# A decoder layer on one core: 192 gathered tokens in place of 160, one-hot rows made four tokens at a time, and three pieces of work moved

## The chip, the core and the metric

The kernel runs on one core of a Trainium2 chip. Its engines are PE (TensorE, matrix products), DVE (VectorE), ACT (ScalarE), POOL (GpSimd) and SP (SyncE, which here only issues transfers); DMA engines move data between the main memory and the core's on-chip memory. The metric is the device time of one execution in microseconds (us), lower is better.

## What is computed

One layer of a decoder on 512 tokens of width 2048, in float32: two attention mixers with a gated merge, a layer norm, then a retrieval over 16,384 single-neuron experts, then a second layer norm. The part that the change touches is the retrieval. Cut to that:

```python
def peer_ffn(h, wq, subkeys, u_tab, v_tab):           # h: 512 x 2048, u_tab and v_tab: 16384 x 2048
    q = (xt @ wq).reshape(T, 8, 2, 128)
    s = einsum('thcd,hcnd->thcn', q, subkeys)           # scores against 128 keys, two halves, 8 heads
    top_s, top_i = top_k(s, 16)
    best_s, best_c = top_k(sums of the two halves' 16 x 16 candidates, 16)
    expert = i1 * 128 + i2                              # 8 x 16 = 128 experts of each token
    gate = softmax(best_s)
    act = gelu(einsum('cd,chkd->chk', xc, u_tab[expert]))
    return einsum('chk,chkd->cd', gate * act, v_tab[expert])
h1 = layer_norm(alpha * x + mix)
x  = layer_norm(alpha * h1 + peer_ffn(h1) + sigmoid(h1 @ ple_gate) * (p @ ple_proj))
```

## The kernel before

All large products are made three times from float32 split into a high and a low part: `mm3` (line 100) issues hi*hi, hi*lo and lo*hi into one sum. `load_split` (line 87) brings 512 KB of weights by SP, makes the high part `whi` on ACT (line 93) and the low part `wlo` on DVE (line 95), or on POOL (line 97) where that is asked for. The three tiles `raw`, `whi` and `wlo` have three buffers each.

The retrieval is done in two ways. For the first T0 = 128 + GX tokens (GX = 32, so 160) each token's 128 experts are **gathered**: 160 columns `k` of expert numbers (HG), one indirect transfer of 128 rows of 2048 floats (1 MB) for each, first from the u table, then from the v table, so 320 steps, and two more that only use what is there. A step (`gather_to`, line 624) issues the transfer of row tile n on POOL's queue (line 599) and lets DVE use row tile n-2: for u a product with the tokens and a sum (line 606), for v a multiply-add into `accg` or `accx` (line 620). There are three row tiles. For the other TD = 352 tokens the retrieval is **dense**: all 16,384 experts are computed for every one of them. The experts come in 128 units of 128; `dense_u` (line 712) makes one unit's products with 48 matmuls whose moving operand has TD columns. Eight units are a group; each result is multiplied by its gate (line 870), split again into `ah` and `al` (lines 873, 874), and the group's product with the v table (line 898) is 384 matmuls of TD columns, whose sums DVE adds into `acc` (line 902). There are 16 groups. The first 32 units' u products (LOOK = 4 groups) are made early, stored in `ad` and fetched again by POOL's queue into tiles `a` (line 866, two buffers).

The work around it, in the order of the program: the output projection `mix`, in two halves of 256 tokens, with the first layer norm of half 0 (`norm1(0)`) after the first four steps of the second half; `half_keys(0)` and `half_keys(1)`, the key search, with dense units in between as filler and, in the second, the first gather steps; `dense_gates` (line 654), which for each dense token makes a 128 x 128 table of gates as the product of two one-hot matrices, 16 tokens to a batch; two filler units and two gather steps go into each batch, the filler being first what is left of the early dense units, then the 32 units of `ple_units`. After that come the last eight of the 32 early units and the groups. `gather_steps` (line 800) spreads the gather steps that are left over 226 calls in the groups. At the end the sums are transposed, added and normalized.

A scheduler sets the order of the instructions on every engine from the program's order and its own estimates of times. `gather_to` asks it to place a step's instructions behind the latest `wlo` on DVE.

## Time and profile before

| what | us |
| --- | --- |
| median of three runs | 4023.78 (4021.25 to 4023.92) |
| profiled execution | 4021.22 |
| its span, first to last instruction | 4019.4 |
| PE busy | 3822.7 (95%) |
| DVE busy | 2704.3 (67%) |
| ACT busy | 1282.2 (32%) |
| POOL busy | 685.3 (17%) |

DMA moved 886.99 MB, on the mean 221 GB/s. A matmul is pipelined, so the duration shown for one (326 ns) is longer than the distance from one to the next; where PE runs without a gap the distance is read from the count of matmuls in a stretch. The profile's rows by stage tell more than the shares of the whole span, since the stages have different limits.

### The profile page before, as it was taken

The page shows a single profiled execution, that of the slowest core. Times are in us where ns is not written, and L with a number is a line of the kernel's source. Part 1 is how long each engine was busy: PE and PEld are TensorE (multiplying, and loading weights), DVE is VectorE, ACT ScalarE, POOL GpSimd, SP SyncE. Part 2 cuts the span into 40 slices and gives each one's busy share as a digit, 9 for nine tenths or more (in the row PEclk, how much of TensorE's full clock was granted, in tenths as well). Part 3 has the DMA queues.
Part 4 walks back from the last instruction along what each step waited for, and adds up shares of the span by engine and source line. Part 5 has one row for each costly group of instructions (what it writes and reads, how often), then busy time and mean ns, then how long its engine had stood idle before and what let it go on. Part 6 is the DMA issues. An engine that isn't in the chain of part 4 may idle for free.

```text
span 4019.4 us, 54040 instructions
## 1 busy us (share of the span) xinstructions
PE 3822.7 (95%) x21545; PEld 3535.9 (88%) x21545; DVE 2704.3 (67%) x4220; ACT 1282.2 (32%) x1660; POOL 685.3 (17%) x493
## 2 busy tenths in 40 slices
PE   8999999999998889979988899999999999999996
PEld 7888877888886789978878898999999999999996
DVE  5344343222257788899996777777777777777877
ACT  3222233222233433334433222333333333333331
POOL 0000000000002355521122222222211211111110
PEclk9999999999999999989998999999999999999998
DMA  4222222222256455658888787888888888888884
GB/s 141 95 89 85 76 74 71 92 95 94 95 190 191 155 163 181 226 199 281 287 292 303 270 304 287 304 324 310 302 323 303 310 316 298 316 310 306 318 300 152
DMA packets 242941, 886.99 MB, mean 221 GB/s; under 512 B 23040, under 2 KB 76416, under 8 KB 198016
## 3 DMA queue, kind: packets, MB, share of 16 engines
q1 hardware_dynamic: 182672, 499.91, 36.8%
q0 software_dynamic: 52672, 375.15, 25.5%
q10 hardware_dynamic: 7344, 8.47, 0.6%
q8 instruction: 169, 2.77, 0.3%
q14 instruction: 84, 0.69, 0.1%
HBM read 841.24 MB, written 41.42 MB: 220 GB/s over the span
## 4 chain that ended last, share of the span: by engine, by line
PE 81%; DVE 11%; DMA 3%; issue 3%; ACT 1%; POOL 1%; POOLq 0%; DVEq 0%; ACTq 0%; SPq 0%
PE hp L101 8%; PE hp L103 8%; PE hp L102 8%; PE vp L101 7%; PE vp L103 7%; PE vp L102 7%; PE ps_g L101 3%; PE ps_g L102 3%; PE ps_g L103 3%; PE pg L673 2%; DVE row L606 2%; PE pg L101 1%; PE pg L102 1%; PE pg L103 1%; DMA a<-ad 1%
## 5 line engine op out<-in xcount | busy, mean ns | idle before, releaser
L101 PE MATMUL vp<-ah,whi_vd 128*128 128x352 f32 x2048 | 657.5, 327 | 29.1 <-ACT ah L873 18.2
L103 PE MATMUL hp<-m_hi,wlo_u 128*128 128x352 f32 x2048 | 665.2, 325 | 20.4 <-DVE wlo_u L95 13.6
L101 PE MATMUL hp<-m_hi,whi_u 128*128 128x352 f32 x2048 | 668.4, 326 | 0.0
L102 PE MATMUL hp<-m_lo,whi_u 128*128 128x352 f32 x2048 | 662.5, 323 | 0.0
L102 PE MATMUL vp<-al,whi_vd 128*128 128x352 f32 x2048 | 662.1, 325 | 0.3 <-DVE al L874 0.3
L103 PE MATMUL vp<-ah,wlo_vd 128*128 128x352 f32 x2048 | 644.7, 326 | 9.8 <-DVE wlo_vd L95 9.8
L93 ACT ACTIVATE whi_vd<-raw_vd 128x1024 fp32r<-128x1024 f32 x256 | 270.4, 1059 | 671.5 <-PE vp L102 469.7
L93 ACT ACTIVATE whi_u<-raw_u 128x1024 fp32r<-128x1024 f32 x256 | 271.0, 1059 | 525.6 <-PE hp L102 309.1
L101 PEld LDWEIGHTS vp<-ah,whi_vd 128*128 128x128 f32 x2048 | 387.8, 191 | 33.6 <-ACT ah L873 20.1
L95 DVE TENSOR_TENSOR wlo_vd<-raw_vd,whi_vd 128x1024 fp32r<-128x1024 f32 x256 | 312.5, 1221 | 142.6 <-ACT whi_vd L93 142.3
L95 DVE TENSOR_TENSOR wlo_u<-raw_u,whi_u 128x1024 fp32r<-128x1024 f32 x236 | 295.3, 1252 | 165.6 <-ACT whi_u L93 164.9
L103 PEld LDWEIGHTS hp<-m_hi,wlo_u 128*128 128x128 f32 x2048 | 386.3, 189 | 22.4 <-DVE wlo_u L95 15.3
L103 PEld LDWEIGHTS vp<-ah,wlo_vd 128*128 128x128 f32 x2048 | 385.5, 190 | 11.2 <-DVE wlo_vd L95 11.2
L102 PEld LDWEIGHTS hp<-m_lo,whi_u 128*128 128x128 f32 x2048 | 390.1, 190 | 0.0
L102 PEld LDWEIGHTS vp<-al,whi_vd 128*128 128x128 f32 x2048 | 388.4, 190 | 0.9 <-DVE al L874 0.8
L101 PEld LDWEIGHTS hp<-m_hi,whi_u 128*128 128x128 f32 x2048 | 388.0, 189 | 0.0
L599 POOL DMA_INDIRECT row<-in_u_rows,eidx x160 | 204.1, 1276 | 816.6 <-DVE row L606 546.8
L599 POOL DMA_INDIRECT row<-in_v_rows,eidx x160 | 193.3, 1208 | 829.7 <-DVE accg L620 648.3
L620 DVE SCALAR_TENSOR_TENSOR accg<-row,act,accg 128x2048 f32<-128x2048 f32 x128 | 300.3, 2346 | 0.4
L606 DVE SCALAR_TENSOR_TENSOR row<-row,h1g 128x2048 f32<-128x2048 f32 x128 | 293.4, 2300 | 0.0
L511 POOL TENSOR_TENSOR h1g<-h1g,lnb 128x2048 f32<-128x2048 f32 x1 | 4.6, 4619 | 1259.5 <-PE ht L499 1259.5
L101 PE MATMUL ps_g<-x_hi,whi_g 128*128 128x512 f32 x512 | 202.9, 396 | 0.0
(332 smaller groups left out, 7387.4 us busy)
## 6 DMA issues: line engine op xcount, KB each, us to landing
raw_u<-in_u_dense SPq DMA_DIRECT2D x256, 512.0 KB, 5.5
raw_vd<-in_v_dense SPq DMA_DIRECT2D x256, 512.0 KB, 5.6
raw_g<-in_w_z SPq DMA_DIRECT2D x64, 512.0 KB, 3.4
raw_wo<-in_w_out SPq DMA_DIRECT2D x64, 512.0 KB, 4.2
raw_wq<-in_w_q SPq DMA_DIRECT2D x64, 512.0 KB, 4.0
gd<-sg SPq DMA_DIRECT2D x22, 1024.0 KB, 7.9
gl<-gd POOLq DMA_DIRECT2D x16, 1408.0 KB, 9.7
raw_pg<-in_w_gate SPq DMA_DIRECT2D x32, 512.0 KB, 5.4
```

What stands on the lines that cost most here:

```text
L93: nc.scalar.activation(hi[:, :n], raw[:, :n], AF.Copy)
L95: last_lo[0] = nc.vector.tensor_sub(lo[:, :n], raw[:, :n], hi[:, :n])
L101: nc.tensor.matmul(ps, whi, mhi, start=start, stop=False, **kw)
L102: nc.tensor.matmul(ps, whi, mlo, start=False, stop=False, **kw)
L103: nc.tensor.matmul(ps, wlo, mhi, start=False, stop=stop, **kw)
L511: nc.gpsimd.tensor_mul(o, o, lnb[:, 0, :])
L599: nc.gpsimd.indirect_dma_start(out=row, out_offset=None, in_=u_rows if n < HG else v_rows, in_offset=bass.IndirectOffsetOnAxis(ap=eidx[:, ...
L606: nc.vector.scalar_tensor_tensor(row, row, 1.0, state["h"][n >= HK], op0=ALU.mult, op1=ALU.mult, accum_out=act[:, n:n + 1])
L620: nc.vector.scalar_tensor_tensor(o, row, act[:, k:k + 1], o, op0=ALU.mult, op1=ALU.add)
L673: nc.tensor.matmul(ps[:, t1 * P:(t1 + 1) * P], o1, o2, start=True, stop=True)
```

## The change

GX goes from 32 to 64, so 192 tokens are gathered (384 row tiles, 386 steps) and 320 are dense (TD = 320). In `dense_gates` the one-hot rows are made four tokens at a time by one comparison each on DVE, and the gate is multiplied in by ACT, one instruction to a token; in each batch three gather steps are issued in place of two. `norm1(0)` is drawn out: its first part stands where all of it stood, its four transposing parts each after three steps of the second half of `mix`. Four of the early dense units (`fill(4)`) go between the key search and the gates. The tiles `a` have four buffers in the last of the early units and in the groups.

```diff
--- before.py
+++ after.py
@@ -22,7 +22,7 @@
 D = 2048
 KB = D // P
 NT = T // P
-GX = 32
+GX = 64
 GE = 8
 T0 = P + GX
 TD = T - T0
@@ -517,9 +517,12 @@
     rest = mix(1)
     for _ in range(4):
         next(rest)
-    for _ in norm1(0):
-        pass
-    for _ in rest:
+    early = norm1(0)
+    next(early)
+    for n, _ in enumerate(rest):
+        if n % 3 == 2:
+            next(early, None)
+    for _ in early:
         pass
 
     pre_q = [load_split(w_q[0][:, u * 1024:(u + 1) * 1024], f"wq0_{u}") for u in range(2)]
@@ -663,17 +666,23 @@
             for t4 in range(4):
                 ps = bank(f"pg{tb}_{b}_{t4}")
                 t0 = b * 16 + t4 * 4
+                def onehot(row, name):
+                    eq = k3.tile([P, 4, P], F32, tag=name, name=f"{name}{tb}_{t0}", bufs=2)
+                    nc.vector.tensor_tensor(
+                        eq, tt[:, row, t0:t0 + 4].unsqueeze(2).to_broadcast([P, 4, P]),
+                        io.unsqueeze(1).to_broadcast([P, 4, P]), op=ALU.is_equal)
+                    return eq
+
+                o1 = onehot(0, "o1")
+                eq = onehot(1, "eq")
                 for t1 in range(4):
                     t = t0 + t1
-                    o1 = k3.tile([P, P], F32, tag="o1", name=f"o1_{tb}_{t}", bufs=8)
-                    nc.vector.tensor_scalar(o1, io, tt[:, 0, t:t + 1], None, op0=ALU.is_equal)
                     o2 = k3.tile([P, P], F32, tag="o2", name=f"o2_{tb}_{t}", bufs=8)
-                    nc.vector.tensor_scalar(o2, io, tt[:, 1, t:t + 1], tt[:, 2, t:t + 1],
-                                            op0=ALU.is_equal, op1=ALU.mult)
-                    nc.tensor.matmul(ps[:, t1 * P:(t1 + 1) * P], o1, o2, start=True, stop=True)
+                    nc.scalar.activation(o2, eq[:, t1, :], AF.Copy, scale=tt[:, 2, t:t + 1])
+                    nc.tensor.matmul(ps[:, t1 * P:(t1 + 1) * P], o1[:, t1, :], o2, start=True, stop=True)
                 if t4 % 2:
                     fill(1)
-                    gather_to(steps[1] + 1)
+                    gather_to(steps[1] + (1 if t4 == 1 else 2))
                 nc.scalar.activation(sg[:, :, t4 * 4:(t4 + 1) * 4].rearrange("p i t -> p t i"),
                                      ps.rearrange("p (t i) -> p t i", i=P), AF.Copy)
             nc.sync.dma_start(gdw[:, :, tb * 8 + b - T0 // 16, :], sg.rearrange("p (g i) t -> p g (i t)", i=GE))
@@ -723,7 +732,7 @@
 
     def look_units(i, pool, n, share):
         for i2 in range(i, i + n):
-            a = pool.tile([P, TD], F32, tag="a", name=f"au{i2}")
+            a = pool.tile([P, TD], F32, tag="a", name=f"au{i2}", bufs=4 if pool is not fpool[0] else 2)
             dense_u(i2, a, share())
             nc.sync.dma_start(ad[i2 // GE][:, i2 % GE, :], a)
             yield
@@ -785,6 +794,7 @@
         yield from ple_units()
 
     units = gate_filler()
+    fill(4)
     for tb in range(1, NT):
         dense_gates(tb)
     fill(32 + LOOK * GE)
@@ -861,7 +871,7 @@
         if g:
             gt = gate_tile(g)
         for e in range(GE):
-            a = ap2.tile([P, TD], F32, tag="a", name=f"a{g}_{e}")
+            a = ap2.tile([P, TD], F32, tag="a", name=f"a{g}_{e}", bufs=4)
             if g < LOOK:
                 nc.gpsimd.dma_start(a, ad[g][:, e, :])
             else:
```

DVE between the key search and the first gates, before: the last lookups (`oh`, `ix`), the transposed indices (`tt`) and the first one-hot rows (`o`).

```order
L574 TENSOR_TENSOR oh_3_0_13295<-bcf_3_13293,io 128x512
L574 TENSOR_TENSOR oh_3_1_13299<-bcf_3_13293,io 128x512
L577 TENSOR_TENSOR oh_3_0_13295<-oh_3_0_13295,tf_3_13288 128x512
L577 TENSOR_TENSOR oh_3_1_13299<-oh_3_1_13299,tf_3_13288 128x512
L579 TENSOR_REDUCE ix<-oh_3_0_13295 128x32
L579 TENSOR_REDUCE ix<-oh_3_1_13299 128x32
L660 COPY tt_13335<-pit_13331 128x384
L669 TENSOR_SCALAR o_1_32_13339<-io,tt_13335 128x128
L671 TENSOR_SCALAR o_1_32_13341<-io,tt_13335 128x128
L669 TENSOR_SCALAR o_1_33_13344<-io,tt_13335 128x128
L671 TENSOR_SCALAR o_1_33_13346<-io,tt_13335 128x128
```

The same place now:

```order
L95 TENSOR_TENSOR wlo_u_1_13552<-raw_u_1_13549,whi_u_1_13551 128x1024
L577 TENSOR_TENSOR oh_3_0_13289<-bcf_3_13287,io 128x512
L577 TENSOR_TENSOR oh_3_1_13293<-bcf_3_13287,io 128x512
L580 TENSOR_TENSOR oh_3_0_13289<-oh_3_0_13289,tf_3_13282 128x512
L580 TENSOR_TENSOR oh_3_1_13293<-oh_3_1_13293,tf_3_13282 128x512
L95 TENSOR_TENSOR wlo_pg_0_13630<-raw_pg_0_13627,whi_pg_0_13629 128x1024
L609 SCALAR_TENSOR_TENSOR row_13086,act<-row_13086,h1g 128x2048
L582 TENSOR_REDUCE ix<-oh_3_0_13289 128x32
L582 TENSOR_REDUCE ix<-oh_3_1_13293 128x32
L95 TENSOR_TENSOR wlo_pg_1_13699<-raw_pg_1_13696,whi_pg_1_13698 128x1024
L609 SCALAR_TENSOR_TENSOR row_13233,act<-row_13233,h1g 128x2048
L609 SCALAR_TENSOR_TENSOR row_13657,act<-row_13657,h1g 128x2048
```

The low parts of dense units (`wlo_u`), of the next filler (`wlo_pg`) and gather steps (`row`) stand among the lookups.

POOL's queue at the border of two of the first groups, before: fetched units (`a`), a group's gates (`gl`) and row tiles (`row`).

```order
L866 DMA a_3_18114<-ad 128x352
L866 DMA a_4_18121<-ad 128x352
L599 DMA row_18216<-in_u_rows,eidx 128x2048
L599 DMA row_18283<-in_u_rows,eidx 128x2048
L866 DMA a_5_18128<-ad 128x352
L866 DMA a_6_18135<-ad 128x352
L599 DMA row_18350<-in_u_rows,eidx 128x2048
L866 DMA a_7_18142<-ad 128x352
L866 DMA a_0_18693<-ad 128x352
L853 DMA gl_18691<-gd 128x2816
```

The same border now:

```order
L876 DMA a_3_17668<-ad 128x320
L602 DMA row_17301<-in_u_rows,eidx 128x2048
L602 DMA row_17368<-in_u_rows,eidx 128x2048
L602 DMA row_17435<-in_u_rows,eidx 128x2048
L876 DMA a_4_17675<-ad 128x320
L602 DMA row_17438<-in_u_rows,eidx 128x2048
L602 DMA row_17505<-in_u_rows,eidx 128x2048
L602 DMA row_17572<-in_u_rows,eidx 128x2048
L602 DMA row_17639<-in_u_rows,eidx 128x2048
L602 DMA row_17642<-in_u_rows,eidx 128x2048
L602 DMA row_17767<-in_u_rows,eidx 128x2048
L876 DMA a_5_17682<-ad 128x320
```

At this border the later fetches of a group stood in ones and twos with one or two row tiles between them; now the fourth tile stands ahead of three row tiles, the fifth ahead of six more, and the sixth (`a_5`) behind these.

DVE in the u half of one of the later groups, before: low parts, gated results (`a`, `al`) and row tiles into `accg`.

```order
L95 TENSOR_TENSOR wlo_u_1_26764<-raw_u_1_26761,whi_u_1_26763 128x1024
L620 SCALAR_TENSOR_TENSOR accg<-row_26723,act,accg 128x2048
L874 TENSOR_TENSOR al_0_26649<-a_0_26584,ah_0_26648 128x352
L95 TENSOR_TENSOR wlo_u_0_26805<-raw_u_0_26802,whi_u_0_26804 128x1024
L870 TENSOR_TENSOR a_1_26655<-a_1_26655,gl_26582 128x352
L874 TENSOR_TENSOR al_1_26720<-a_1_26655,ah_1_26719 128x352
L95 TENSOR_TENSOR wlo_u_1_26835<-raw_u_1_26832,whi_u_1_26834 128x1024
L620 SCALAR_TENSOR_TENSOR accg<-row_26726,act,accg 128x2048
L95 TENSOR_TENSOR wlo_u_0_26876<-raw_u_0_26873,whi_u_0_26875 128x1024
```

The same place of a later group now:

```order
L95 TENSOR_TENSOR wlo_u_1_26319<-raw_u_1_26316,whi_u_1_26318 128x1024
L623 SCALAR_TENSOR_TENSOR accg<-row_26208,act,accg 128x2048
L95 TENSOR_TENSOR wlo_u_0_26363<-raw_u_0_26360,whi_u_0_26362 128x1024
L623 SCALAR_TENSOR_TENSOR accg<-row_26281,act,accg 128x2048
L880 TENSOR_TENSOR a_1_26284<-a_1_26284,gl_26211 128x320
L95 TENSOR_TENSOR wlo_u_1_26393<-raw_u_1_26390,whi_u_1_26392 128x1024
L623 SCALAR_TENSOR_TENSOR accg<-row_26352,act,accg 128x2048
L95 TENSOR_TENSOR wlo_u_0_26434<-raw_u_0_26431,whi_u_0_26433 128x1024
L884 TENSOR_TENSOR al_1_26349<-a_1_26284,ah_1_26348 128x320
L95 TENSOR_TENSOR wlo_u_1_26464<-raw_u_1_26461,whi_u_1_26463 128x1024
L623 SCALAR_TENSOR_TENSOR accg<-row_26355,act,accg 128x2048
```

In a later group 19 row tiles stood on DVE beside 32 low parts, 16 gated results and 16 sums; now 22 or 23 do, the rest is unchanged in number.

## Rows read from the trace of the kernel before

**Rows 1.** Busy time by stage: PE, PEld, DVE, ACT, POOL, clock, DMA share, GB/s.

```profile
1240.00:1310.00 70.00, 54.94 (x241) 43.37 (x240) 53.46 (x62) 26.45 (x37) 22.66 (x10) 0.90 0.60 185
1450.00:1750.00 300.00, 287.82 (x2060) 286.04 (x2060) 250.55 (x720) 109.22 (x149) 165.18 (x72) 0.98 0.62 199
1750.00:1790.00 40.00, 14.85 (x78) 14.30 (x77) 35.05 (x120) 8.70 (x11) 1.89 (x2) 0.66 0.40 135
1790.00:2080.00 290.00, 279.63 (x1519) 242.81 (x1518) 262.98 (x676) 120.19 (x126) 41.33 (x47) 0.98 0.86 283
2080.00:2140.00 60.00, 46.55 (x207) 39.60 (x207) 58.01 (x163) 23.21 (x24) 18.28 (x14) 0.72 0.84 300
2140.00:2200.00 60.00, 59.62 (x375) 59.33 (x373) 37.68 (x33) 20.99 (x25) 12.68 (x10) 1.00 0.87 322
2200.00:2495.00 295.00, 260.43 (x1528) 254.64 (x1529) 214.12 (x266) 81.14 (x97) 71.47 (x73) 0.95 0.77 283
2495.00:3920.00 1425.00, 1425.00 (x8874) 1425.00 (x8873) 1106.77 (x1027) 473.32 (x566) 280.00 (x231) 1.00 0.85 311
```

**Rows 2.** Timeline of PE, first and last of 48 matmuls of 256 columns.

```profile
1609.18 0.28 PE L101 MATMUL ps_wq<-m_hi,whi_wq 128*128 128x256 f32 x1
...
1614.76 0.28 PE L103 MATMUL ps_wq<-m_hi,wlo_wq 128*128 128x256 f32 x1
```

**Rows 3.** Groups by form, 2510 to 3910: count, busy us, mean ns, idle us.

```profile
L620 DVE SCALAR_TENSOR_TENSOR accg<-row,act,accg 128x2048 f32<-128x2048 f32 x128 | 300.3, 2346 | 0.4
L95 DVE TENSOR_TENSOR wlo_u<-raw_u,whi_u 128x1024 fp32r<-128x1024 f32 x187 | 228.6, 1223 | 106.1 <-ACT whi_u L93 105.6
L902 DVE TENSOR_TENSOR acc<-acc,vp 128x352 f32<-128x352 f32 x176 | 88.7, 515 | 59.9 <-PE vp L103 59.9
L874 DVE TENSOR_TENSOR al<-a,ah 128x352 fp32r<-128x352 f32 x93 | 48.7, 524 | 40.1 <-ACT ah L873 40.1
L599 POOL DMA_INDIRECT row<-in_v_rows,eidx x160 | 193.3, 1208 | 829.7 <-DVE accg L620 648.3 <-DVE accx L620 141.8 <-DMA row<-in_v_rows,eidx 13.0
```

**Rows 4.** DMA, 2510 to 3910: packets; gather queue; landing time of a row tile.

```profile
DMA packets 85119, 434.34 MB, mean 310 GB/s; under 512 B 9464, under 2 KB 9464, under 8 KB 55935
q0 software_dynamic: 32737, 242.64, 47.3%
row<-in_v_rows,eidx POOLq DMA_INDIRECT x160, 7.7
```

**Rows 5.** Timeline at the first norm: start, duration, engine, line.

```profile
1260.78 4.62 POOL L511 TENSOR_TENSOR h1g<-h1g,lnb 128x2048 f32<-128x2048 f32 x1 [1259.46 <-PE ht L499]
1266.40 4.83 DVE L505 TENSOR_TENSOR m_lo<-ht,m_hi 128x256 fp32r<-128x256 f32 x1
1271.76 8.74 DVE L505 TENSOR_TENSOR m_lo<-ht,m_hi 128x256 fp32r<-128x256 f32 x2
```

**Rows 6.** One-hot rows by form, comparison of 512 elements, ACT on 128 columns.

```profile
L671 DVE TENSOR_SCALAR o<-io,tt 128x128 f32<-128x128 f32 x336 | 113.8, 339 | 0.0
L669 DVE TENSOR_SCALAR o<-io,tt 128x128 f32<-128x128 f32 x336 | 93.8, 279 | 11.3 <-PE pg L673 11.2
1768.77 1.24 DVE L574 TENSOR_TENSOR oh<-bcf,io 128x512 f32<-128x512 f32 x2
L260 ACT ACTIVATE p<-p,nm 128x128 f32<-128x128 f32 x32 | 12.4, 387 | 0.0
```

**Rows 7.** Waits, 2190 to 2460: us in total, times, longest.

```profile
PE vp L101 <- ACT ah L873: 18.2, 6, 5.0
POOL row L599 <- DVE row L606: 137.7, 26, 8.3
DVE a L870 <- DMA a<-ad: 33.9, 8, 7.5
```

**Rows 8.** DMA, 2140 to 2200: landing time of a row tile.

```profile
row<-in_u_rows,eidx POOLq DMA_INDIRECT x8, 9.1
```

**Rows 9.** Busy time in ten us of the output projection, columns as in 1.

```profile
1150.00:1160.00 10.00, 10.00 (x45) 8.11 (x44) 2.46 (x3) 2.12 (x2) 0.00 (x0) 1.00 1.00 404
```

## The prediction

> **What bounds the kernel now.** I read first the busy time by stage [rows 1], then the groups of one stage by form, then the waits where PE is not full. From 2495 to 3920 PE is busy for all of 1425 us at the full clock; DVE has 1106.77 us of work there (78%) and DMA moves 311 GB/s at a share of 0.85. This stage, most of groups 4 to 15, is bound by PE alone, and two other engines have about a fifth and a seventh to spare. Ahead of it PE is not full: it lacks 15 us of the 70 at the first norm (1240 to 1310), 25 of the 40 between key search and gates (1750 to 1790, at a clock of 0.66), 10 and 13 us in the gates (1790 to 2140), and 35 of the 295 in the first groups (2200 to 2495). In the key search (1450 to 1750) DVE is busy for 250.55 of 300 us and PE for 287.82. So a shorter product is worth its full size only after 2140, and up to the point at which DVE or DMA is full.
>
> **The columns.** In the PE-bound stage 8874 matmuls of 352 columns take 1425 us, 160.6 ns each [rows 1]. At 256 columns, 47 distances take 1614.76 - 1609.18 = 5.58 us, 118.7 ns [rows 2]. The line between the two gives 146.6 ns at 320 columns: 14.0 ns less. No weight load stands in the way down to 256. There are 128 units of 48 and 16 groups of 384 such matmuls, 12,288 in all, so at most 12,288 x 14.0 ns = 172 us. By stage: 960 matmuls in the key search (13 us), the four moved units (192, 3 us), the last eight early units with groups 0 to 3 (1920, 27 us), groups 4 to 15 (9216, 129 us).
>
> **What the 64 further steps cost.** A step is 2.35 us of DVE [rows 3] (2.28 and a read of the sum for u rows) and 1.05 MB of DMA: 64 x 2.35 = 150 us and 67 MB. 16 of them fall into the gates, the rest behind. None is on PE; what they cost is what they take from the two spare shares.
>
> **Groups 4 to 15.** A group is 768 matmuls: 768 x 160.6 ns = 123.3 us now, 112.6 after. DVE in a group after: 32 low parts x 1.223 = 39.1; 16 sums x 0.48 = 7.7 and 16 gated results x 0.49 = 7.8 (0.515 and 0.524 now [rows 3], shortened by a sixteenth, since 32 of 352 columns go); 22.4 row tiles x 2.35 = 52.6. Sum 107.2 of 112.6 us, 95%. Before it is 39.1 + 8.2 + 8.3 + 19 x 2.35 = 100 of 123. DMA after: 32 loads of 0.524 MB = 16.8, 22.4 rows = 23.5, a gate tile 1.3, together 41.6 MB, which in 112.6 us is 369 GB/s. The mean of 310 GB/s [rows 4] at a share of 0.85 [rows 1] gives 365 GB/s at a full share, so 41.6 MB need 114 us; ten us of the output projection show 404 GB/s at a full share [rows 9], which gives 103. Row tiles: three buffers, and a buffer's round is the issue on POOL with the landing, 7.7 us [rows 4], 1.21 us of POOL [rows 3] ahead of it and 2.35 us of use: 11.3 us for three rows, 3.8 us a row, while 112.6 / 22.4 = 5.0 is allowed. But landing takes 9.1 us where 322 GB/s move [rows 8, 1]; at 11.5 us it is 22.4 x 15.05 / 3 = 112.4, the bound itself. So four limits lie between 103 and 114 us, and a queue that is full to 95% on three engines does not run at its bound. Bounds of a group: 113 (PE and a us of stalls) and 123 (nothing gained). I take 117, nearest to the DMA row at its own share. 12 x (123.3 - 117) = **76 us** gained, between 0 and 124.
>
> The Trainium skill (DMA: Bandwidth & Descriptors, section Specifications) gives about 358 GB/s as what one core may draw from main memory. By that a group needs 41.6 / 0.358 = 116 us, an estimate from that page, 2 us more than by the row's share, or 24 us over twelve groups; the 404 GB/s of [rows 9] speak against so low a ceiling, at least for ten us.
>
> **The last early units and groups 0 to 3** (2140 to 2495, 355 us). 1920 x 160.6 ns = 308 us, so 47 are lost. The waits [rows 7] show how: PE waits for `ah` (18.2 us, six times, the borders of groups), DVE for the fetched `a` (33.9), and POOL, which issues those fetches, for a row tile to come free (137.7). With two `a` tiles a group's eight need four rounds of fetch and split at a border where only one `ah` is free ahead; with four, two rounds. Against it, 11 row tiles stand in a group of 56 us in place of 9 or 10 in 62, and six of them now ahead of `a_5` on POOL's queue. I leave 30 of the 47 us: 1920 x 146.6 ns = 281 + 30 = 311, **44 us** gained; bounds 10 (more lost at the borders than now) and 65.
>
> **Key search to gates.** The four units, 192 x 146.6 ns = 28 us of PE, now stand where PE lacks 25 us and runs at 0.66; their eight low parts (9.8 us of DVE) stand among the lookups, the first gates wait longer by that, and filler units follow them on PE. I leave 8 us of gap, so 36 us go by. The gates lose those units (31 us of PE) and 32 of 352 tokens. One-hot rows: 339 + 279 ns on DVE for each of 352 tokens [rows 6], 218 us; now 160 comparisons of 512 elements, of which two take 1.24 us [rows 6], so 0.62 each, 99 us. ACT gains 320 products of 128 columns, 0.39 us at most (an exponential with a sum [rows 6]), 125 us beside the 143 that it has in this stage [rows 1]: room in 350. DVE: 321 - 218 + 99 + 16 x 2.35 - 9.8 = 230. But DMA is at 0.86 and 0.84 [rows 1], 300 us of work in 350; 16 more rows are 16.8 MB / 365 GB/s = 46, eight fewer loads and two fewer batches stored (1 MB each) take 17 off: 329 us. So in the gates DMA takes the place of DVE, and the stage needs about 340, after 36 ahead of it: 376 against the 390 from 1750 to 2140. With the better rate of [rows 9] PE and its unfed last batches decide, some 345 in all. I take **18 us** gained, bounds 0 and 45.
>
> **The first norm.** POOL's work on `h1g` and `y` begins at 1260.78, as soon as the transposes are done, and holds up DVE: two `m_lo`, each a quarter of a `wlo` in size, take 8.74 us, another 4.83 [rows 5], the `wlo` behind them is late, and PE stands still. Drawn out, the transposes end later and POOL's work, which waits for the last of them, meets low parts with slack of two loads ahead. It blocks DVE all the same, elsewhere. **12 us** gained of the 15, bounds 0 and 18.
>
> **Key search:** 13 us of shorter products in a stage where DVE is nearly full; **6 us**, bounds 0 and 13. **The end:** PE's last products lie in groups 4 to 15; two `up` tiles fewer are hidden behind them. 0.
>
> **Sum.** 76 + 44 + 18 + 12 + 6 = 156 us. The profiled execution took 4021.22 us, 2.6 below the median; against the median 4023.8 - 156 = **3868 us**.
>
> **Rivals.** (A) PE stays the only bound: groups at 113.7 (115 us), 60 in the first groups, 40 at the gates, 15 and 9 at norm and search: 4024 - 239 = 3785. For it: in DVE's order of a later group the low parts that are needed next still stand ahead of the sums that wait for PE. Against it: 369 GB/s would have to last 1350 us, and the stage now has 311. (B) DVE and DMA take PE's place wholly and groups stay at 122 to 123: 80 us from the other stages and some 4 here, 3940. For it: DVE is in order, and a row tile that has not landed holds up the low parts behind it. (C) Slower: row tiles land so late under the higher rate that the three buffers set the pace. The price is 22.4 x (landing + 3.55) / 3 a group; with 80 us gained elsewhere it turns into a loss over 130 us a group, at a landing of 13.8 us. At 15 us: 138.5, twelve times 15.2 = 182 lost, 4024 + 182 - 80 = 4126. For it, 7.7 rises to 9.1 us between 311 and 322 GB/s; against it, fewer bytes a us move as soon as it happens. (D) The shorter product isn't faster (a matmul held by its weight load): only the moves count, 12 + 15 + 17 us, 3980; against it, the 118.7 ns of [rows 2].
>
> **Chances.** My sum 0.63, A 0.11, B 0.16, C 0.07, D 0.03. The range must hold 0.8: my own case reaches from 3815 to 3930, and with most of B and the near part of A it is 3795 to 3945. About 0.2% is what a measurement of this kernel can tell from no change. Faster: all but C and a little of B and D, 0.91; slower 0.07; the same 0.02.
>
> **What would show it.** Groups 4 to 15: the distance of matmuls 146.6 ns where PE is full; PE idle of 2 to 6 us a group, before L103 on a `wlo`; DVE at 90 to 95%; DMA over 0.9 at 350 GB/s; landing of rows 8 to 11 us. Under A, PE has no idle there and landing stays at 8; under B and C, PE's idle is over 8 us a group, and row tiles wait for their transfer on DVE. Gates: DMA share over 0.92, DVE near 230 us. 1750 to 1790: no gap over 10 us. First groups: PE waiting for `ah` under 15 us. Wrong I would be above all if DMA can't pass 340 GB/s for long (groups at 122), or passes 390 with ease (groups at 113).

## The result and the profile after

The changed kernel takes 3910.36 us (median of 4 runs, 3906.61 to 3915.72) where the kernel before takes 4022.52 (4 runs of the same comparison, 4014.12 to 4023.92): a ratio of 0.9726, with a 95% interval from 0.9708 to 0.9745. That is 112 us less. Forecast were 156 us less, 3868 us, in a range from 3795 to 3945. The profiled execution of the changed kernel took 3908.73 us, with a span of 3907.0.

To see where the time went, both programs are cut at the same events: the end of the output projection, of the key search, the first and the last product of the gates, the first product of the second expert half (`vp`) of group 0, and the ends of groups 3, 7, 14 and 15. Busy time by stage of the kernel before at these cuts; the columns are stretch, length, then busy us (instructions) of PE, PEld (TensorE's weight loads), DVE, ACT and POOL, TensorE's granted clock (1.00 is full speed), DMA share, GB/s:

```profile
1345.99:1744.45 398.46, 358.73 (x2602) 355.08 (x2602) 344.94 (x978) 143.97 (x206) 226.43 (x95) 0.96 0.56 182
1744.45:1777.77 33.32, 8.96 (x61) 8.68 (x59) 31.70 (x105) 7.53 (x11) 1.89 (x2) 0.71 0.45 151
1777.77:2141.54 363.77, 339.16 (x1789) 295.08 (x1790) 329.89 (x869) 146.41 (x153) 59.61 (x60) 0.92 0.84 278
2141.54:2204.62 63.08, 58.08 (x363) 57.79 (x362) 39.83 (x37) 22.39 (x27) 14.72 (x12) 0.98 0.90 330
2204.62:2496.39 291.77, 261.82 (x1537) 256.03 (x1537) 212.74 (x263) 80.35 (x94) 69.44 (x72) 0.96 0.76 283
2496.39:2989.76 493.37, 493.37 (x3075) 493.37 (x3074) 379.31 (x393) 162.02 (x193) 105.25 (x82) 1.00 0.85 313
2989.76:3853.04 863.28, 863.28 (x5377) 863.28 (x5377) 676.09 (x590) 286.01 (x339) 163.24 (x140) 1.00 0.85 309
3853.04:3988.20 135.16, 130.92 (x809) 129.96 (x808) 106.09 (x108) 39.92 (x48) 11.50 (x9) 0.97 0.70 241
```

The changed kernel at the same events:

```profile
1320.77:1718.86 398.09, 350.58 (x2603) 346.57 (x2602) 345.04 (x973) 143.62 (x206) 226.17 (x95) 0.94 0.56 181
1718.86:1772.08 53.22, 37.46 (x253) 36.19 (x251) 49.94 (x121) 18.91 (x26) 7.09 (x5) 0.89 0.65 218
1772.08:2110.17 338.09, 295.37 (x1512) 254.21 (x1513) 286.02 (x342) 212.53 (x451) 91.31 (x73) 0.91 0.91 318
2110.17:2175.58 65.41, 56.58 (x385) 56.05 (x384) 43.83 (x40) 22.59 (x27) 22.04 (x16) 0.96 0.93 345
2175.58:2445.88 270.30, 242.78 (x1539) 235.37 (x1540) 219.75 (x274) 79.00 (x93) 89.33 (x75) 0.96 0.86 327
2445.88:2930.11 484.23, 460.36 (x3071) 451.79 (x3071) 401.07 (x414) 159.53 (x193) 140.51 (x96) 1.00 0.91 347
2930.11:3745.34 815.23, 798.73 (x5376) 788.35 (x5376) 713.61 (x613) 282.66 (x340) 224.99 (x163) 1.00 0.94 358
3745.34:3878.22 132.88, 121.16 (x806) 118.92 (x806) 107.01 (x110) 39.89 (x49) 19.20 (x12) 0.95 0.75 269
```

| stage | before, us | after, us | gained | forecast |
|---|---|---|---|---|
| to the end of the output projection | 1346.0 | 1320.8 | 25.2 | 12 |
| key search | 398.5 | 398.1 | 0.4 | 6 |
| key search to last gate | 397.1 | 391.3 | 5.8 | 18 |
| last early units, groups 0 to 3 | 354.9 | 335.7 | 19.2 | 44 |
| groups 4 to 7 | 493.4 | 484.2 | 9.2 | 25 |
| groups 8 to 14 | 863.3 | 815.2 | 48.1 | 44 |
| group 15 | 135.2 | 132.9 | 2.3 | 6 |
| end | 31.2 | 28.8 | 2.4 | 0 |

(The forecast for groups 4 to 15 was 6.3 us a group; the table splits it.) So the later groups came as forecast, the stages between key search and group 7 fell short by 53 us, and the first stage gave 13 us more than forecast, 7 more than its bound of 18 allows. That last number is the strangest, for of that stage the change touches only the last 110 us.

In groups 8 to 14 the changed kernel is no longer bound by TensorE alone. It needs 815.2 / 7 = 116.5 us a group where 768 products of 146.6 ns are 112.6; DVE is busy for 713.6 of 815 us, DMA has a share of 0.94 and moves 358 GB/s. In [rows 1] the later groups had 0.85 and 311 GB/s. The transfers in that stretch, time from issue to landing last:

```profile
row<-in_v_rows,eidx POOLq DMA_INDIRECT x157, 8.6
raw_vd<-in_v_dense SPq DMA_DIRECT2D x112, 512.0 KB, 7.3
```

A row lands after 8.6 us where it took 7.7 [rows 4]. In groups 4 to 7 the share is 0.91. In groups 0 to 3 it is 0.86, and of all groups it is there that PE lacks most, 27.5 of 270.3 us.

### The profile page after: what moved, and what is told of

It is laid out like the page before. It is cut to its first block, busy times and chain, and to the rows that moved or that the text cites. A ratio compares the mean times of both kernels' runs of the same rounds, so it can differ in the third digit from the quotient of the medians.

```text
span 3907.0 us, 54029 instructions
## 1 busy us (share of the span) xinstructions
PE 3646.7 (93%) x21481; PEld 3361.2 (86%) x21481; DVE 2752.3 (70%) x3766; ACT 1352.6 (35%) x1972; POOL 852.9 (22%) x555
## 5 line engine op out<-in xcount | busy, mean ns | idle before, releaser
L103 PE MATMUL hp<-m_hi,wlo_u 128*128 128x320 f32 x2048 | 639.1, 314 | 44.9 <-DVE wlo_u L95 36.9
L101 PE MATMUL vp<-ah,whi_vd 128*128 128x320 f32 x2048 | 629.0, 312 | 27.7 <-ACT whi_vd L93 15.9
L102 PE MATMUL vp<-al,whi_vd 128*128 128x320 f32 x2048 | 630.4, 311 | 7.9 <-DVE al L884 7.9
L101 PE MATMUL hp<-m_hi,whi_u 128*128 128x320 f32 x2048 | 637.6, 312 | 0.0
L102 PE MATMUL hp<-m_lo,whi_u 128*128 128x320 f32 x2048 | 635.4, 310 | 0.0
L103 PE MATMUL vp<-ah,wlo_vd 128*128 128x320 f32 x2048 | 605.8, 314 | 29.3 <-DVE wlo_vd L95 28.9
L602 POOL DMA_INDIRECT row<-in_u_rows,eidx x192 | 296.8, 1546 | 745.7 <-DVE row L609 697.0
L602 POOL DMA_INDIRECT row<-in_v_rows,eidx x192 | 269.0, 1401 | 722.8 <-DVE accg L623 464.9
L101 PEld LDWEIGHTS vp<-ah,whi_vd 128*128 128x128 f32 x2048 | 387.6, 190 | 31.4 <-ACT whi_vd L93 18.7
```

The source lines that it names most:

```text
L101: nc.tensor.matmul(ps, whi, mhi, start=start, stop=False, **kw)
L102: nc.tensor.matmul(ps, whi, mlo, start=False, stop=False, **kw)
L103: nc.tensor.matmul(ps, wlo, mhi, start=False, stop=stop, **kw)
L602: nc.gpsimd.indirect_dma_start(out=row, out_offset=None, in_=u_rows if n < HG else v_rows, in_offset=bass.IndirectOffsetOnAxis(ap=eidx[:, ...
```

## Experiments

**Whose is the pace of the first 1200 us?** Up to there the change touches nothing, yet the products of 512 columns follow each other faster after it: 1732 of them in 400 us before (231 ns), 1767 after (226 ns). Five kernels were run to tell. The first is the kernel before, unaltered:

> The kernel before itself, once more, on the chip that the next three kernels use. In the first 1200 us the change touches nothing, yet the products of 512 columns follow each other at 232.7 ns in the trace of before and at 227.0 ns in that of after, and after is some 23 us ahead by 1200 us. If this pace belongs to the run (the chip or the moment), this run may show any value between the two, the same as the other three kernels of this call, and the 23 us are no gain of the change. If it belongs to the program, this run shows 232.7 ns again, the output projection ends at 1346 us, and the kernels that carry the change's code show 227.0. Time against before: 1.000 in both cases, within 0.2% if the pace belongs to the program.

Measured: 4019.46 us, ratio 1.000 (0.999 to 1.001), and the old pace, with the projection's end at 1345.7 us. Its busy time from 700 to 1100 us:

```profile
700.00:1100.00 400.00, 400.00 (x1732) 324.44 (x1732) 115.13 (x118) 90.34 (x105) 0.00 (x0) 1.00 0.30 94
```

The second kernel is the one before with the columns alone:

```diff
-GX = 32
+GX = 64
```

> The kernel before with 64 tokens of the second block gathered in place of 32 and nothing else of the change (two gather steps in a batch of the gates, two buffers for a, one-hots token by token, first norm in one piece). Own theory (transfers at about 358 GB/s are the limit of the later groups): more rows are left for the groups, about 23.7 in place of 22.4 in each later one, 43 MB or 120 us, so 12 x 3 = 36 us gained there; the gates lose 32 of 352 tokens, 30 us; the first groups 5 to 10 us; together 70 to 80 us against before. Rival (the number of columns alone decides, rows are hidden): groups at 113 to 114 us, 120 us gained there and 160 in all. Second rival (a group's length is set by VectorE's queue): 23.7 x 2.35 + 54.6 = 110 us of VectorE in a group, groups at 122 and 50 us gained in all.

It has the new pace, and its projection ends at 1321.2 us. The third is the changed kernel with `GX = 32`, so the rest alone:

> The changed kernel with 32 tokens of the second block gathered in place of 64: all of the change but the shorter product and the further rows. Own theory: groups 4 to 15 are bound by TensorE alone again, 123.3 us each, nothing gained there; norm 0 to 3 us, key search to the end of the gates 10 to 20 us, first groups 5 to 15 us (three gather steps in a batch leave 17.4 rows for a later group, 8.7 for a first one); together 15 to 35 us against before. Rival (the moves matter more than the columns): over 45 us. Second rival (the moves cost): slower than before by up to 10 us.

It has the old pace, and 1345.3 us. (Their times are told below.) So the pace belongs to the program, and to `GX`. What `GX` alters ahead of 1200 us is one thing: the three small gather tiles `lg`, `eidx` and `act` (`P + GX` words a partition, in the first pool) grow by 128 bytes each, and every tile behind that pool moves up by 384 bytes. The next kernel is the kernel before with that shift and nothing else:

```diff
     act = gp.tile([P, HG], F32, name="act")
+    pad = gp.tile([P, 96], F32, name="pad")
+    nc.vector.memset(pad, 0.0)
```

> The kernel before with one unused tile of 384 bytes a partition behind the three small gather tiles, so that the loaded weights and all that stands behind them lie where the changed kernel has them; nothing else is changed. If the addresses set the pace: 227.0 ns at 512 columns, the output projection ends at 1321 us in place of 1346, and 20 to 25 us less in all (ratio 0.994 to 0.995). If the pace comes from another part of the change to 192 tokens: 232.7 ns, 1346 us, ratio 1.000.

Measured: 3980.75 us (3980.34 to 3985.46), ratio 0.991 (0.9896 to 0.9923). 38 us by an unused tile. The projection ends at 1323.4 us, and from 700 to 1100 us:

```profile
700.00:1100.00 400.00, 400.00 (x1766) 331.31 (x1766) 116.43 (x119) 92.13 (x108) 0.00 (x0) 1.00 0.30 96
```

Most of the rest of the 38 us lies in the groups: groups 8 to 14 take 856.0 us in place of 863.3, so the 5376 products of 352 columns come at 159.2 ns in place of 160.6. The last kernel of this kind makes products alone, at chosen addresses:

> A kernel that computes nothing of the layer: streams of 96 products each, as the kernel makes them, from one large tile, so that every operand stands at a chosen address. The weight tiles (for the output projection the tiles that are streamed) stand at the addresses of the kernel before plus 0, 64, 128 and so on up to 448 bytes (letters a to h in the names); the kernel before has 0 (a), the changed one 384 (g). Forms: gate (512 columns, weights from the loaded tiles), out (512 columns, loaded tiles streamed), key (256), unit (320, first expert product), late (320, second expert product, streamed tiles 32 bytes off a multiple of 64), even (the same, on a multiple of 64). If the addresses set the pace: gate and out at 232.7 ns in a and 227.0 in g, key at 118.7 in a and 120.0 in g, and the other letters show which addresses are best, between 215 and 235 ns at 512 columns. If something else of the program sets it: the same distance in all eight letters of a form.

Measured, as the distance of the products in ns (start of a stream to start of the next, by its 96 products; in the very first, gate at a, the trace shows 94 in the stretch from 161.18 to 183.12 us, so there by 94):

| form, columns | a, +0 | b, +64 | c, +128 | d, +192 | e, +256 | f, +320 | g, +384 | h, +448 |
|---|---|---|---|---|---|---|---|---|
| gate, 512 | 233.4 | 228.9 | 226.9 | 233.3 | 232.2 | 228.9 | 226.9 | 233.3 |
| out, 512 | 233.2 | 233.3 | 226.7 | 229.1 | 233.2 | 233.3 | 226.7 | 229.1 |
| key, 256 | 120.0 | 117.8 | 119.9 | 113.5 | 120.0 | 117.8 | 119.9 | 113.5 |
| unit, late, even, 320 | 146.7 | 146.7 | 146.7 | 146.7 | 146.7 | 146.7 | 146.7 | 146.7 |

The rows of c and d from PE's timeline (start, length of the stream, name, count):

```profile
357.20 21.94 PE L41 MATMUL gatec<-big 128*128 128x512 f32 x96
378.98 21.92 PE L41 MATMUL outc<-big 128*128 128x512 f32 x96
400.74 11.68 PE L41 MATMUL keyc<-big 128*128 128x256 f32 x96
412.25 14.24 PE L41 MATMUL unitc<-big 128*128 128x320 f32 x96
426.33 14.25 PE L41 MATMUL latec<-big 128*128 128x320 f32 x96
...
454.50 22.56 PE L41 MATMUL gated<-big 128*128 128x512 f32 x96
476.90 22.15 PE L41 MATMUL outd<-big 128*128 128x512 f32 x96
498.89 11.07 PE L41 MATMUL keyd<-big 128*128 128x256 f32 x96
509.79 14.24 PE L41 MATMUL unitd<-big 128*128 128x320 f32 x96
523.87 14.25 PE L41 MATMUL lated<-big 128*128 128x320 f32 x96
```

From `gatec` to `outc` are 21.78 us for 96 products, from `gated` to `outd` 22.40; from `keyc` to `unitc` 11.51, from `keyd` to `unitd` 10.90; the streams of 320 columns are equal. So the pace depends on where the loaded tiles stand (the activations stood still), and it does so at 512 and 256 columns but not at 320. It repeats every 256 bytes: a and e, b and f, c and g, d and h agree within 0.1 ns in every form but gate at a and e, which are 1.2 apart. The kernel before stands at a, the changed one at g, which with c is the fastest place for 512 columns. Not every number is the kernel's own: at a the gate form gives 233.4 here and 232.7 in the kernel's trace, but 256 columns 120.0 here and 118.7 there [rows 2]. How an address makes a product slower was not tested.

**The parts apart.** The kernel with the columns alone took 3967.57 us, ratio 0.9874 (0.9858 to 0.9891), 52 us less, of which 24.5 us are the pace. The kernel with the rest alone took 4001.27, ratio 0.9954 (0.9938 to 0.9971), 18 us less. Together they are 70, and the change gave 112: 42 us come only from the two at once. Groups 8 to 14 show how. The columns alone:

```profile
2948.38:3794.97 846.59, 810.86 (x5375) 795.68 (x5375) 732.20 (x623) 282.12 (x338) 253.10 (x173) 0.99 0.94 355
```

846.6 us for 166 rows, 121 us a group, where the changed kernel has 156 rows and 815.2. DMA has a share of 0.94 in both, with 355 and 358 GB/s. 10 rows are 31 us apart, 3.1 us each, and a row of 1.05 MB at 355 GB/s is 3.0 us. With the rest alone, groups 8 to 14 take 862.8 us, the 863.3 of before, although fewer rows stand there: TensorE alone bounds them. So a row that is moved ahead is worth nothing with 352 columns and three us with 320. What the rest of the change costs and brings shows in the traces of the columns alone and of the whole: from the end of the key search to the first `vp` they take 426.6 and 456.7 us, 30.1 more for the whole, and the whole is shorter by 32.5 us in groups 0 to 3, by 14.0 in 4 to 7 and by 31.4 in 8 to 14.

The third gather step was taken out of the changed kernel:

```diff
-                    gather_to(steps[1] + (1 if t4 == 1 else 2))
+                    gather_to(steps[1] + 1)
```

> The changed kernel with two gather steps in a batch of the gates, as before, in place of three. Some 20 rows more are left for the groups: about 23.6 in a later one, 42.9 MB, which at 357 GB/s are 120 us. If the place of the rows is what the three steps bring (own theory): the end of the gates 20 to 28 us earlier than in the changed kernel, groups 4 to 15 at 122 to 124 in place of 119.4, the first groups some 10 us longer, in all 20 to 45 us slower than the changed kernel. Rival (a row costs the same wherever it stands): within 8 us of the changed kernel. Second rival (transfers have room): 15 us or more faster.

Measured: 3938.62 us (3933.61 to 3943.08), ratio to before 0.9799 (0.9782 to 0.9816), 28 us slower than the changed kernel. The gates end 15 us earlier, with 38 rows in them for 57, and groups 8 to 14 have 166 rows again:

```profile
2937.51:3777.28 839.77, 806.93 (x5375) 792.44 (x5374) 733.91 (x622) 281.19 (x338) 253.48 (x173) 0.99 0.94 359
```

That is 24.5 us more than in the changed kernel, and groups 4 to 7 take another 16.6 more: what the gates give back is lost almost three times over in the groups.

**Transfers or VectorE?** Both are near full in the later groups. In the changed kernel, some groups were to use a row tile that is already there, and some to gather rows without using them:

```diff
+        if 34 <= n - HG < 101:
+            rows[n] = rows[n - 1] if n - 1 in rows else state["keep"]
+            state["keep"] = rows[n]
+            return
...
         k = n - HG
+        if 101 <= k < 168:
+            return
```

> The changed kernel with two stretches of later groups altered: about three groups (8 to 10) use one row tile that is already there, so that the v rows of these steps are not gathered (23.5 MB a group less DMA, VectorE as before); about three more (11 to 13) gather their rows but leave out the addition on VectorE (52 us a group less VectorE, DMA as before). The output is not the layer's. A whole group is 116.5 us in the changed kernel, 112.6 us of it products. If the transfers are the limit: 113 to 114 us in the first stretch, 116 to 117 in the second. If VectorE's queue is: 116 to 117 in the first and 113 to 114 in the second. If the two only bind together: 113 to 114 in both.

This run did not tell them apart: with nothing to wait for, the unused gathers ran ahead into the groups without gathers, and both loads stood in the same stretch, 117 to 125 us a group. It showed that transfers can run at 371 to 374 GB/s and a share of 0.97 for 240 us when the gathers don't wait for VectorE. The second try keeps a short use, `o, row = o[:, 0:16], row[:, 0:16]`, in place of the `return`:

> The test of the two limits of a later group again, since in the run before it the gathers without use moved ahead into the stretch without gathers, and both stood together at 117 to 125 us with transfers at 371 GB/s. Now about three groups (near 8 to 10) use a row tile that is already there (no gather, VectorE as before), and about three (near 11 to 13) gather their rows and use 16 columns of each in place of 2048 on VectorE, so that the tiles come free as before. The output is not the layer's. If the transfers are the limit: 113 to 114 us without gathers, 116 to 117 with short uses. If VectorE's queue is: 116 to 117 without gathers, 113 to 114 with short uses. If only the two together: 113 to 114 in both.

Busy time by stage: two groups without gathers (the cut between them lies 3 us early), then three with gathers and short uses, of which the last has 10 full uses among its 23:

```profile
3052.30:3162.00 109.70, 109.70 (x750) 109.70 (x749) 98.72 (x85) 38.75 (x48) 0.55 (x1) 1.00 0.52 161
3162.00:3277.60 115.60, 115.60 (x791) 115.60 (x790) 101.44 (x89) 40.53 (x49) 0.53 (x1) 1.00 0.52 162
3390.20:3504.70 114.50, 113.37 (x770) 112.68 (x769) 58.29 (x92) 42.19 (x51) 24.38 (x23) 1.00 0.95 366
3504.70:3621.20 116.50, 115.01 (x771) 114.22 (x770) 56.14 (x87) 41.25 (x49) 26.39 (x23) 0.99 0.93 353
3621.17:3734.42 113.25, 113.25 (x770) 112.63 (x769) 74.56 (x86) 38.71 (x47) 26.43 (x23) 1.00 0.94 361
```

The first two take 225.3 us together, 112.65 each, PE busy in all of it, with DVE at 99 and 101 us: without transfers of rows TensorE is the only bound, at VectorE's full load. The other three take 114.5, 116.5 and 113.3 us, with DVE at 58, 56 and 75 of the 102 that a group has in the changed kernel. Of the 3.9 us that a group of the changed kernel takes beyond its products, all go without the transfers, and 2.1 stay on the mean of these three with less work on VectorE. So nothing is lost without the transfers, and VectorE alone costs nothing; beside them its work costs about two us more. This is between the first and the last of the three outcomes expected, and with three groups from 0.6 to 3.8 us the split is rough.

**One more row tile.** If the transfers had gaps for want of a buffer, a fourth tile would fill them:

```diff
-    LEAD = 2
+    LEAD = 3
...
-            a = pool.tile([P, TD], F32, tag="a", name=f"au{i2}", bufs=4 if pool is not fpool[0] else 2)
+            a = pool.tile([P, TD], F32, tag="a", name=f"au{i2}", bufs=3 if pool is not fpool[0] else 2)
...
-            a = ap2.tile([P, TD], F32, tag="a", name=f"a{g}_{e}", bufs=4)
+            a = ap2.tile([P, TD], F32, tag="a", name=f"a{g}_{e}", bufs=3)
```

> The changed kernel with four row tiles in place of three (three gathers ahead of their use), and three buffers for a in place of four, for the room. In the first groups GpSimd waits 204 us and in groups 4 to 7 252 us for VectorE to free a row tile, while the transfers have shares of 0.87 and 0.91. If the transfers are kept short by the missing buffer: first groups at 62 to 64 us in place of 67, groups 4 to 7 at 117 to 118 in place of 122, 25 to 35 us less than the changed kernel in all. If the transfers or VectorE are at their limit: within 6 us of the changed kernel. Rival: one more gather in flight delays the weights, up to 15 us slower.

Measured: 3923.45 us (3912.35 to 3929.96), ratio 0.977 (0.9755 to 0.9785), 13 us slower at the medians. The profiled execution is the fastest of the four. In it groups 4 to 7 take 484.2 us, as in the changed kernel; the first groups 280.6 in place of 270.3, with one of the four buffers of `a` given up for it. So the row buffer is not what holds groups 4 to 7 at a share of 0.91. What does was not found.

**The buffers for `a`, and the four units.** Two parts that lie in different stages were undone in one kernel:

```diff
-            a = pool.tile([P, TD], F32, tag="a", name=f"au{i2}", bufs=4 if pool is not fpool[0] else 2)
+            a = pool.tile([P, TD], F32, tag="a", name=f"au{i2}", bufs=2)
...
-    fill(4)
     for tb in range(1, NT):
...
-            a = ap2.tile([P, TD], F32, tag="a", name=f"a{g}_{e}", bufs=4)
+            a = ap2.tile([P, TD], F32, tag="a", name=f"a{g}_{e}")
```

> The changed kernel with two undone parts that lie in different stages: two buffers for a in place of four, and no four units ahead of the gates. Prediction for the buffers: 17 of the 44 us of the first groups, so 10 to 25 us more from the last gate to the end of group 3. Rival: no more than 5 us, the fetches are hidden. Prediction for the four units: they fill a gap of 25 us, so 12 to 20 us more from the end of the key search to the last gate. Rival: the units only push the one-hots back and VectorE decides, then within 5 us.

Measured: 3932.7 us (3922.26 to 3950.38), ratio 0.978 (0.9759 to 0.9801), 22 us slower than the changed kernel. From the key search's end to the first gate, to the last gate, to the first `vp`, and to the end of group 3 (the profiled execution is the slowest of the four):

```profile
1724.39:1756.33 31.94, 8.26 (x60) 8.02 (x59) 31.30 (x97) 7.98 (x13) 1.89 (x2) 0.66 0.45 153
1756.33:2097.32 340.99, 317.12 (x1704) 276.24 (x1705) 299.07 (x354) 220.38 (x463) 87.99 (x74) 0.95 0.94 330
2097.32:2169.29 71.97, 58.91 (x385) 57.61 (x384) 46.64 (x45) 22.96 (x28) 23.21 (x17) 0.95 0.92 334
2169.29:2467.71 298.42, 252.00 (x1540) 242.92 (x1541) 221.02 (x274) 78.95 (x93) 89.99 (x77) 0.92 0.79 297
```

Groups 0 to 3 take 298.4 us with two buffers and 270.3 with four: 28 us, more than forecast. Some of it may belong to this execution, which also takes 9 us longer in groups 4 to 7 and 11 in 8 to 14. But between the kernel before and the rest alone, with 352 columns in both and 37 and 34 rows there, the same groups differ by 31.7 us (291.8 and 260.1). From the end of the key search to the first `vp`, however, it is 444.9 us without the four units ahead and 456.7 with them: that part of the change costs 12 us where 15 were to be gained. The two kernels differ in the buffers of `au`, the early units' tiles, there too, so the 12 us are for both. A kernel without the four units and with all the rest was not run.

**The one-hot rows** were made token by token again in the changed kernel (the old loop in place of `onehot` and the activation):

> The changed kernel with the one-hot rows made token by token on VectorE, as before. VectorE's one-hots then take 320 x (339 + 279 ns) = 198 us in place of 108. In the kernel with the columns alone, 40 rows and these one-hots, the gates took 328 us; 17 rows more are 40 us of VectorE. If VectorE limits the gates (own theory now, against the prediction's transfers): 360 to 370 us from the first gate to the last in place of 338, 20 to 32 us slower than the changed kernel in all. If the transfers limit them, as predicted: 338 to 345, under 8 us.

Measured: 3926.38 us (3915.92 to 3942.42), ratio 0.9786 (0.9758 to 0.9814), 16 us slower at the medians, 7 in the profiled executions. The gates:

```profile
1768.76:2120.58 351.82, 309.91 (x1544) 266.93 (x1545) 333.69 (x823) 129.45 (x133) 98.11 (x74) 0.89 0.91 311
```

351.8 us where the changed kernel has 338.1, between what the two theories gave. DVE has 334 us there and 286 with the new one-hots, DMA a share of 0.91 in both. With less work on VectorE beside the same rows the gates are 13.7 us shorter, so VectorE binds for a part of the stage. That the transfers bind for the rest is likely at their share of 0.91 but not shown, since the kernel with fewer rows relieves both. Why the saving on DVE is 48 us and not the 90 of the expectation, the timeline of DVE shows. Before, for one token and the next (start, duration):

```profile
1900.17 0.28 DVE L669 TENSOR_SCALAR o<-io,tt 128x128 f32<-128x128 f32 x1
1900.37 0.34 DVE L671 TENSOR_SCALAR o<-io,tt 128x128 f32<-128x128 f32 x1
1900.63 0.28 DVE L669 TENSOR_SCALAR o<-io,tt 128x128 f32<-128x128 f32 x1
```

and for eight tokens after, with the operation behind them:

```profile
1901.64 1.29 DVE L671 TENSOR_TENSOR o<-tt,io 128x512 f32<-128x512 f32 x2
1902.84 1.31 DVE L671 TENSOR_TENSOR eq<-tt,io 128x512 f32<-128x512 f32 x2
1904.07 1.21 DVE L95 TENSOR_TENSOR wlo_pg<-raw_pg,whi_pg 128x1024 fp32r<-128x1024 f32 x1
```

The durations are 0.28 and 0.34 us, 0.62 a token, but the next operation begins before the one ahead has ended: from 1900.17 to 1900.63 is one token, 0.46 us. After, two comparisons of each kind, eight tokens, take from 1901.64 to 1904.07, 0.30 us a token. For 320 tokens that is 50 us saved.

**The stop at the first norm.** In [rows 5] two small operations of DVE take 8.74 us under GpSimd's work. In the changed kernel the transposes are drawn out from 14.3 us (1246.1 to 1260.5) to 28.1 (1222.8 to 1250.9), and GpSimd's work begins 70 us ahead of the projection's end in place of 85. The stop of PE is still there, 11.77 us for 12.96. DVE at that place (start, duration, and what):

```profile
1249.61 0.42 DVE L505 TENSOR_TENSOR m_lo<-ht,m_hi 128x256 fp32r<-128x256 f32 x1
...
1251.90 5.00 DVE L95 TENSOR_TENSOR wlo_wo<-raw_wo,whi_wo 128x1024 fp32r<-128x1024 f32 x1
1256.83 9.43 DVE L505 TENSOR_TENSOR m_lo<-ht,m_hi 128x256 fp32r<-128x256 f32 x2
1266.18 6.64 DVE L95 TENSOR_TENSOR wlo_wo<-raw_wo,whi_wo 128x1024 fp32r<-128x1024 f32 x2
```

GpSimd's first and last operation there:

```profile
1251.20 4.62 POOL L511 TENSOR_TENSOR h1g<-h1g,lnb 128x2048 f32<-128x2048 f32 x1 [1249.88 <-PE ht L499]
...
1265.94 4.67 POOL L512 TENSOR_TENSOR y<-y,lnb 128x2048 f32<-128x2048 f32 x1
```

One `m_lo` takes 0.42 us at 1249.61; the two at 1256.83 take 9.43, and of three low parts of 1.22 us one takes 5.00 and two take 6.64 together. From 1251.9 to 1272.8, beside GpSimd's work from 1251.2 to 1270.6, VectorE does these five operations, which are 4.5 us by their usual size. The Trainium skill (SBUF — State Buffer, section SBUF: two separate sides) says that a VectorE operation with two inputs in the on-chip memory and a GpSimd operation that reads it lock each other out, for the whole of an instruction. The trace agrees: low parts have two such inputs, and each waits for an operation of 4.6 to 5.6 us. If so, GpSimd's help is dearer than the work, which led to a version that might beat both kernels:

```diff
-        nc.gpsimd.tensor_mul(o, o, lnb[:, 0, :])
-        nc.gpsimd.tensor_add(o, o, lnb[:, 1, :])
+        nc.vector.tensor_mul(o, o, lnb[:, 0, :])
+        nc.vector.tensor_add(o, o, lnb[:, 1, :])
```

> A try at a better version: the changed kernel with the scaling of the normed rows (8 operations of 128 x 2048) on VectorE in place of GpSimd. In the trace of the changed kernel the stop of 11.8 us at the first norm is still there: while GpSimd has 19 us of that work, four operations of VectorE, 4.1 us by their usual size, take 21 us. If GpSimd's work holds VectorE up: stop under 4 us, output projection ends at 1309 to 1314 us in place of 1321, and the key search is no longer than now, since 18 us of VectorE replace 38 us of hold-up: 8 to 20 us less in all. Rival (the eight operations of 2.3 us cost the key search what they save): within 5 us.

Measured: 3891.37 us (3889.13 to 3895.89), ratio to before 0.9687 (0.9669 to 0.9704), 19 us less than the changed kernel, whose runs all lie above it. DVE at the same place:

```profile
1251.80 2.28 DVE L511 TENSOR_TENSOR h1g<-h1g,lnb 128x2048 f32<-128x2048 f32 x1
...
1254.45 2.28 DVE L511 TENSOR_TENSOR y<-y,lnb 128x2048 f32<-128x2048 f32 x1
1256.65 1.22 DVE L95 TENSOR_TENSOR wlo_wo<-raw_wo,whi_wo 128x1024 fp32r<-128x1024 f32 x1
1257.79 0.42 DVE L505 TENSOR_TENSOR m_lo<-ht,m_hi 128x256 fp32r<-128x256 f32 x1
1258.12 2.28 DVE L512 TENSOR_TENSOR h1g<-h1g,lnb 128x2048 f32<-128x2048 f32 x1
```

Each of the eight operations takes 2.28 us, the low parts 1.22 again; PE's longest stop is 1.1 us, the projection ends at 1308.7 us for 1320.8, and the key search is no longer, 395.8 us for 398.1 (396.5 to 401.2 in the other kernels with 320 columns, so this difference is no gain shown). The other us between the two lie behind, in stages that this edit doesn't touch.

## Why the forecast came out as it did

The range held and the direction was right; the gain was 112 us of 156, and a good part of it did not come from where it was said to come. Step by step:

- **The columns** were right: 146.6 ns was the line between two points, 146.7 is measured at every address, and two groups that nothing else holds take 112.65 us for the 112.6 worked out. That the 160.6 ns of before held 1.4 ns of address was not seen.
- **Groups 8 to 14** were right: 117 forecast, 116.5 measured, and by the mechanism named, transfers and VectorE both near full beside TensorE. Without the transfers nothing is lost. The size was in part a choice: 114 us were worked out from bytes, the three on top of it were not. The transfers run at 358 GB/s over 815 us. The 358 GB/s of the Trainium skill (DMA: Bandwidth & Descriptors, section Specifications), which the prediction set against the 404 of [rows 9], are what this stretch of 815 us shows; as a ceiling they do not hold, with 371 to 374 for 240 us in one run.
- **Groups 4 to 7 and 15**: here the step failed that took one length for all twelve groups. Groups 4 to 7 need 121 us at a share of 0.91, with 89 rows and 1.5 MB more for the sums that start there; group 15 is longer by its own end in both kernels. 20 us less were gained than said; why groups 4 to 7 need more than the later ones stays open.
- **The first groups**: 19 us for 44. The failing step is that no bytes were summed for them, as they were for a later group. 16 loads (8.4 MB), eight fetches and a gate tile (2.6) and 43 / 4 rows (11.3) are 22.3 MB in the 56.3 us of their products, 396 GB/s; by 358 GB/s such a group needs 62 us. The late loads show in the waits: ScalarE, which splits the v table's weights as they land, waits 105.5 us for them in these groups, and 33.1 before. But the transfers have 327 GB/s and 0.86 there, and a group takes 67.6 us; the 5 us beyond 62 are not explained. The buffers for `a`, 17 us in the prediction, were worth about 30 by the two comparisons above; with the columns alone these four groups became longer, 302.8 us against 291.8, with 46 rows in them for 37.
- **Key search to gates**: 6 us for 18. The gates were forecast at 340 us and took 338, but by luck: VectorE was put at 230 us and has 286, since 0.62 us a token was a sum of durations and the distance is 0.46, and the transfers, put at 329 us of work, have 308 (0.91 of 338). Ahead of the gates, the four units were to leave 8 us of gap and 36 in all; it is 53, with a stop of 14.5 us. The step failed that took the gap for one of TensorE's: DVE is busy for 49.9 of the 53.2 us, and with low parts and rows added ahead of the one-hots the first gate comes later. The prediction named that cost ("the first gates wait longer by that") and left it out of the sum. Against the kernel with the columns alone, which needs 358.8 us from the end of the key search to the last gate, the moves cost 32.5 us here: 17.6 go with the third gather step, 18.4 with the four units and the buffers of `au`; the new one-hots give back about 10, and 7 are not accounted for.
- **The first norm**: the 12 us are not there: the kernel with the norm in one piece and the new addresses ends its projection at 1321.2 us, the changed one at 1320.8, and kernels that are equal up to there differ by 3. The failing step is the slack "of two loads ahead" that the low parts were to have. The hold-up was known ("it blocks DVE all the same, elsewhere"), and elsewhere was no better.
- **Key search**: 0.4 of 6 us. The step failed that let half of the 13 us of shorter products through. At the same addresses the stage takes 400.1 us with 352 columns (the kernel with the unused tile) and 399.5 with 320 (the columns alone), which is no difference beyond the scatter, and VectorE is busy for 345 us of it before and after. Its products of 256 columns also went from 118.7 to 120.0 ns with the new addresses.
- **Missing altogether**: the 24.5 us by the addresses in the first 1346 us. They are luck: without them the gain would have been about 87 us, 3935, still in the range but next to rival B.

Of the rivals, A (no idle on PE) and D (no shorter product) are excluded by 116.5 us and 146.7 ns. C never came near: rows land after 8.6 us, and 13.8 was its point. B gave 3940 and is the nearest: its sign, over 8 us of idle a group, is nearly there in groups 4 to 7 (8.5 us beyond the products, 6.0 of them idle on PE by the profile) and not after them (3.9 and 2.4). Of the other signs, DMA over 0.9, rows landing in 8 to 11 us and a wait for `ah` under 15 us (10.4) came; DVE in groups 8 to 14 (88%), the gates (0.91, 286 us) and the gap ahead of them (a stop of 14.5 us) did not. Against a kernel before with the same addresses (ratio 0.991), the change is worth 0.9726 / 0.991 = 0.981.

## What to carry over

Sum the bytes of every stage at its new, shorter time, not of the longest one alone; work moved ahead is worth its price only where that resource binds. Take an engine's cost for a run of short operations from the distance of their starts, not from the sum of their durations. And when a change alters the size of a tile, compare the pace of products in a stage that it doesn't touch before crediting the change with the whole difference: an unused tile of 384 bytes was worth 38 us here.

## What was not expected of the hardware

Products of 512 columns took 226.7 to 233.4 ns and products of 256 columns 113.5 to 120.0, by the address of the loaded tile modulo 256 bytes against fixed activations; products of 320 columns took 146.7 at all eight places. Under GpSimd's operations of 4.6 to 5.6 us, VectorE's low parts of 1.22 us took up to 5.0; the same eight operations on VectorE take 2.28 us each and made the kernel 19 us faster.
